# Stores of ScalarE's results begun from ScalarE's queue, and z's first two token blocks side by side

## The chip, the cores and the metric

The kernel runs on one core of a Trainium2 chip. The core has a matrix engine (TensorE, PE in the profile), three engines for elementwise work (VectorE or DVE, ScalarE or ACT, GpSimd or POOL), a queue engine (SyncE or SP) that here only begins transfers, and 16 DMA engines that move data between the chip's memory (HBM) and the core. Every engine works through its own list of instructions in the order in which the program gives them; a semaphore makes an instruction wait for another engine's result. A DMA is begun by an instruction on some engine's list, and that engine goes on as soon as the transfer is handed over.

The metric is the device time of one execution in microseconds (us). Three runs of the kernel before gave 1551.68, 1552.48 and 1552.88 us, so the median is 1552.48 us.

## What is computed

One layer of a decoder with two token mixers side by side, 1024 tokens of width 1024, all in float32:

```python
h = rms_norm(x, norm_w)
q, k, v, z_a, xbc, z_s, dt_raw, gate_logits = split(h @ w_in)   # 1024 x 11296
# branch A: attention with two softmax maps per head, 8 heads
y_a = diff_attention(q, k, v, ...) * silu(z_a)
# branch B: a state space scan in chunks of 128 tokens, 32 heads in 4 groups
xbc = silu(causal_depthwise_conv(xbc, conv_w, conv_b))
y_s = ssd_chunked(xs, dt, A, B, C, D)
y_s = gated_group_rms_norm(y_s, z_s, ssd_norm_w)                 # y * silu(z_s)
# merge
g_a, g_s = split(gate_logits)
merged = sigmoid(g_a) * (y_a @ w_proj_attn) + sigmoid(g_s) * (y_s @ w_proj_ssd)
out = x + merged @ w_out
```

Nearly all the time goes into the matrix products with w_in, w_proj_attn, w_proj_ssd and w_out. Each float32 factor is split into a high and a low part of a faster format, and a product is three matmuls: high times high, high times low, low times high.

## The kernel before

**A planner writes the order.** The kernel's Python code holds a small model of the engines (class Plan). Each step is a generator that emits instructions and yields the time at which it wants to go on; the planner keeps a clock for TensorE (pl.t) and one each for ScalarE ("A"), VectorE ("V"), GpSimd ("G"), SP's queue ("Q") and the DMA engines ("D"), and runs whatever is due. So the order of instructions on every engine's list is fixed when the program is built, by the model's costs. The function load (line 278) begins every DMA of the kernel but two, loads and stores alike, on SP's list. A store is emitted at the model's time at which its data are done.

**The front.** Tokens are worked on in eight blocks of 128 (t = 0 to 7). prep_h normalises a block: a square sum on ScalarE, a root on GpSimd, a scaling on VectorE, eight 128x128 transposes on TensorE (ph in the profile), then h_evac copies the high part to hH on ScalarE and the low part to hL on VectorE. The first products are those of z (z_first, line 1299; "y0" in the list of the order, FRONT_ORDER): for a token block t it multiplies the first half of the inner dimension (four slices kb, 12 matmuls, called "half 0" here) into a bank of PSUM; z_copy (line 1323) then copies that sum to a tile zc on ScalarE and stores it; then the second half (12 more matmuls, "half 1") is added in the same bank, and z_evac (line 1476) applies Silu and stores the result. The second half may not begin before the copy is done, since it goes on adding in the bank that is being read. Kept sums serve the later products of z by a scheme with seven products in place of eight (z_part, z_step), which fetch zc from HBM and may put changed sums back (z_keep, line 1334).

For the first pair of columns (pr = 0) z_first works on the blocks in the order (0), (1), (2, 3): block 0 alone, block 1 alone, blocks 2 and 3 together. Together means half 0 of both, then half 1 of both. After the first group it starts consts, which loads twelve small tables through SP's queue.

**Later stages.** From about 88 us to 540 us follow the products of gates (front_pair with kind g, gate_step), of the convolution's input (kind c; conv, line 1444) and the remaining products of z; from about 330 us the scan (ssd_core, ssd_chunk) runs beside them and goes on beside the attention (att_proj, att_block) from 557 us; then the last gates (gates, gate_evac) to about 1237 us, the products with w_proj (products) and with w_out (final).

**The stores that the change touches.** In att_block the tile yt (attention's result, transposed, last written on ScalarE); in z_keep the tile zc, from z_copy last written by ScalarE, and from z_step the tiles zu and zv last written by VectorE; in conv the tile cv after its Silu on ScalarE; in z_evac the tile zs or zu after its Silu; in gate_evac the tile gt after its Tanh. There are 48 stores of cv, 32 of z_evac, 24 of z_keep, 16 of yt and 12 of gt, each of 128 x 512 float32 (256 KB).

In front_pair a bank is used again after ScalarE has copied it: product p = 1 fills a bank, ScalarE copies it to fc, product p = 6 follows in another bank, and p = 2 goes on in the first one, which needs the copy ("ct").

Of the kernel before, what the change touches and what calls it, by code (L numbers as in the profile page):

```python
# [15 lines left out]
P = 128  # L16
# [137 lines left out]
def tile_hybrid_layer(ctx: ExitStack, tc: tile.TileContext, x, norm_w, w_in, q_norm_w, k_norm_w,  # L154
                      diff_lambda, subln_w, conv_w, conv_b, dt_bias, a_log, d_skip, ssd_norm_w,
                      w_proj_attn, w_proj_ssd, w_out, out):
    nc = tc.nc
# [14 lines left out]
    ya_d = dram.tile([1024, S], F32, name="ya_d")  # L172
    ys_d = dram.tile([2048, S], F32, name="ys_d")
    gt_d = dram.tile([2048, S], F32, name="gt_d")
    act_d = dram.tile([NT, SH, P], F32, name="act_d")
    acc_d = dram.tile([2048, 512], F32, name="acc_d")
    cv_d = dram.tile([3072, S], F32, name="cv_d")
    z_d = dram.tile([GROUPS, S, 512], F32, name="z_d")
# [3 lines left out]
    zc_d = dram.tile([2, 2, 512, 512], F32, name="zc_d")  # L182

    pl = Plan()
# [10 lines left out]
    def midt(shape=(P, 512), dt=F32, name="m"):  # L195
        return mid.tile(list(shape), dt, tag="b2", name=name)
# [39 lines left out]
    def pe_done():  # L236
        return pl.t + DONE
# [11 lines left out]
    def act(o, i, f, after, **kw):  # L249
        nc.scalar.activation(o, i, f, **kw)  # L250
        if f in (AF.Silu, AF.Exp) and f != table[0]:
            table[0] = f
            pl.op("A", 1.3, after)
        c = 0.83e-3 * i.free_size() + (0.052 if in_ps(i) else 0.093) + 0.093 * (("accum_out" in kw) + any(not isinstance(kw.get(i, 0.0), float) for i in ("scale", "bias")))
        return pl.op("A", c, after)
# [9 lines left out]
    def stt(o, a, s, b, op0, op1, after):  # L265
        nc.vector.scalar_tensor_tensor(out=o, in0=a, scalar=s, in1=b, op0=op0, op1=op1)
        sb = not in_ps(a, b)
        return pl.op("V", 0.07 + 0.07 * sb + 1.042e-3 * o.free_size() + (0.0 if isinstance(s, float) else 0.06), after, sb)
# [6 lines left out]
        nc.vector.tensor_copy(o, a)  # L275
        return pl.op("V", 0.065 + (1.042e-3 if in_ps(a) else 0.52e-3) * o.free_size(), after)

    def load(o, i, after=0.0):
        nc.sync.dma_start(out=o, in_=i)
        q = pl.op("Q", 0.48, max(after, pl.t))  # L280
        n = o.free_size() * 512 / 360e3 if o.space != bass.MemoryType.DRAM else i.free_size() * 512 / 360e3
        return pl.op("D", n, q + 0.6) + lag[1]

    def rsqrt(dst, src, add, after):
        cols = src.free_size()
        if isinstance(add, float):
            nc.gpsimd.tensor_scalar(out=dst, in0=src, scalar1=add, scalar2=None, op0=ALU.add)
        else:
            nc.gpsimd.tensor_tensor(out=dst, in0=src, in1=add, op=ALU.add)
        nc.gpsimd.tensor_tensor(out=dst, in0=dst, in1=mhalf[:, 0:cols], op=ALU.pow)  # L290
        return pl.op("G", 0.55 + 0.18 * cols, after)
# [100 lines left out]
    for kind, i in ORDER1:  # L392
# [8 lines left out]
        elif kind == "z":  # L401
            pr, p = divmod(i, 10)
# [196 lines left out]
    def w_next(n):  # L599
        i = used[0]  # L600
        used[0] += n
        return list(range(i, i + n))

    def w_need(i):
        while i not in w_at:
            yield pl.t + 0.1
        while w_at[i] > pl.t:
            yield w_at[i]

    def w_done(i):  # L610
        ws.give(w_slot[i], pl.t + 0.1)
        wts.pop(i)

    def wide(i):
        return wts[i][:, 0].rearrange("p f c -> p (f c)"), wts[i][:, 1].rearrange("p f c -> p (f c)")
# [5 lines left out]
    def steps3(o, a, b, first, last, **kw):  # L621
        mm(o, a[0], b[0], first, False, **kw)
        yield
        mm(o, a[0], b[1], False, False, **kw)
        yield
        mm(o, a[1], b[0], False, last, **kw)
        yield
# [215 lines left out]
    def hblk(kb, t):  # L843
        return hH[:, kb, t * P:(t + 1) * P], hL[:, kb, t * P:(t + 1) * P]
# [83 lines left out]
    def att_block(h, qb, pk, scs):  # L928
        v, zg, kk, ks = hd[h]
        n = (qb + 1) * P  # L930
# [32 lines left out]
        pr, sums = zip(*[got[m] for m in range(2)])  # L963
        at = max(ex)
# [6 lines left out]
        at = max(t1, t2)  # L971
        yield at
        nc.gpsimd.tensor_tensor(out=cc, in0=rec, in1=n0, op=ALU.mult)
        at = pl.op("G", 0.25, at)
        yield at
        at = stt(pr[0][:, 0:n], pr[1][:, 0:n], cc, pr[0][:, 0:n], ALU.mult, ALU.add, at - HOP)
# [30 lines left out]
        at = pe_done()  # L1007
# [4 lines left out]
        at = act(y, av[:, 0:P], AF.Square, at, accum_out=ss)  # L1012
        yield at
        f = tin(1, "f")
        at = rsqrt(f, ss, e1, max(at, t_e))
        yield at
        at = stt(y, av[:, 0:P], f, zg[:, qb, :], ALU.mult, ALU.mult, at)
# [13 lines left out]
        yt = yts[qb // 4]  # L1031
# [3 lines left out]
        at = pe_done()  # L1035
        yield at
        sms.give(kx, at)
        at = act(yt[0][:, (qb % 4) * P:(qb % 4 + 1) * P], py[:, 0:P], AF.Copy, at, scale=sub_c)
        trs.give(k, at)
        yt[2] += 1  # L1040
        if yt[2] == 4:
            yield at
            at = load(ya_d[h * P:(h + 1) * P, qb // 4 * 512:qb // 4 * 512 + 512], yt[0], at)
            ytm.give(yt[1], at)
            ready.setdefault("att", []).append(at)

# [251 lines left out]

    def z_first(pr):
        ids = w_next(KB)  # L1300
        for ts in (((0, 1), (2, 3)) if pr else ((0,), (1,), (2, 3))):
            pms = []
            for t in ts:
                k = yield from pl.get(trs, first=True)
                pms.append((mmt(f"pmz{pr}{t}"), k))
            for half in range(2):
                for t, (pm, k) in zip(ts, pms):
                    while half and (pr, t) not in z_c:
                        yield pl.t + 0.1
                    for kb in range(half * 4, half * 4 + 4):  # L1310
                        yield from w_need(ids[kb])
                        while (t, half) not in h_at:
                            yield pl.t + 0.1
                        while h_at[t, half] > pl.t:
                            yield h_at[t, half]
                        yield from steps3(pm, hblk(kb, t), wide(ids[kb]), kb == 0, kb % 4 == 3, skip_group_check=True)
                        if t == 3:
                            w_done(ids[kb])
                    pl.spawn(z_evac(2 * pr, t, pm, k, False) if half else z_copy(pr, t, pm), pe_done())
            if pr == 0 and ts[0] == 0:  # L1320
                pl.spawn(consts())

    def z_copy(pr, t, pm):
        at = pe_done()
        km = yield from pl.get(mids)
        c = midt(name=f"zc{pr}{t}")
        at = act(c, pm, AF.Copy, at)
        z_c[pr, t] = at
        yield at
        z_keep(pr, 0, t, c, km, at, False)  # L1330
# [2 lines left out]

    def z_keep(pr, n, t, o, km, at, keep):
        if not keep:
            at = load(zc_d[pr, n, t * P:(t + 1) * P], o, at)
            mids.give(km, at)
            o = None
        z_u[pr, n, t] = (o, km, at)
# [104 lines left out]
    def conv(b, h, ps, cell, at, free=None):  # L1444
        km = yield from pl.get(mids)
        cv = midt(name=f"cv{h}")
        yield max(at, pl.t)
        if h == 0:
            tail = tin(3, "tail")
            cell["tail", b] = (tail, act(tail, ps[:, 509:512], AF.Copy, at))  # L1450
        at = act(cv, ps, AF.Identity, at, bias=cbc(b), scale=cwc(3, b))
        for j in (1, 2, 3):
            yield at
            yield from pl.room("V")
            at = stt(cv[:, j:512], ps[:, 0:512 - j], cwc(3 - j, b), cv[:, j:512], ALU.mult, ALU.add, at)
        if h:
            while ("tail", b) not in cell:
                yield pl.t + 0.1
            tail, t = cell["tail", b]
            at = max(at, t)  # L1460
            for j in (1, 2, 3):
                yield at
                yield from pl.room("V")
                at = stt(cv[:, 0:j], tail[:, 3 - j:3], cwc(3 - j, b), cv[:, 0:j], ALU.mult, ALU.add, at)
        yield at
        if free:
            free[0].give(free[1], at)
        at = act(cv, cv, AF.Silu, at)
        cell["conv", b, h] = at
        yield at  # L1470
        at = load(cv_d[b * P:(b + 1) * P, h * 512:h * 512 + 512], cv, at)
        mids.give(km, at)
        cv_at[b, h] = at


    def z_evac(g, t, pm, k, own, at=None):
        at = pe_done() if at is None else at
        if own:
            zz, km = own
        else:  # L1480
            km = yield from pl.get(mids)
            zz = midt(name=f"zs{g}{t}")
        at = act(zz, pm, AF.Silu, at)
        trs.give(k, at)
        yield at
        at = load(z_d[g, t * P:(t + 1) * P, :], zz, at)
        mids.give(km, at)
        z_at[g, t] = at

# [221 lines left out]
    def gate_evac(ob, n, pm, k):  # L1711
        at = pe_done()
        km = yield from pl.get(mids)
        gt = midt(name=f"gt{ob}{n}")
        at = act(gt, pm, AF.Tanh, at, scale=0.5)
        trs.give(k, at)
        yield at
        at = load(gt_d[ob * P:(ob + 1) * P, n * 512:(n + 1) * 512], gt, at)
        mids.give(km, at)


# [529 lines left out]
```

## Time and profile before

| | |
|---|---|
| median of three runs | 1552.48 us |
| the profiled execution's own time | 1552.03 us |
| its span, first to last instruction | 1550.0 us |
| TensorE busy | 1534.9 us, 99% |
| VectorE busy | 1131.5 us, 73% |
| ScalarE busy | 887.6 us, 57% |
| GpSimd busy | 806.9 us, 52% |
| moved by DMA | 289.56 MB, 187 GB/s on average |

All times below are counted from the start of the span. The profile calls an instruction by its engine, its line in the kernel, the operation and the tiles that it writes and reads ("zc<-pmz"). A line can be that of a helper: L250 is every ScalarE operation, L218 every matmul, L279 every DMA begun through load. "Busy" for TensorE is what the trace models: matmuls overlap, and the distance from one start to the next tells the pace. The idle time of an engine is put down to what released it. Instructions that only begin a DMA are listed under the queue (SPq, ACTq) and are not counted as busy.

### The profile page before, as it was taken

The numbers are of one execution on the slowest core, as the hardware profiler recorded it, in microseconds if no ns is written. First come the engines' busy times: TensorE is split into PE (matmuls) and PEld (weight loads), VectorE is DVE, ScalarE is ACT, GpSimd is POOL, SyncE is SP. The second block draws the span as 40 slices with busy tenths as digits, with TensorE's granted clock in tenths as the row PEclk, the third lists the DMA queues.
The fourth block names the chain that finished last, engine by engine and source line by source line (L and its number), as shares of the span: only waits on it lengthen the run. The fifth ranks groups of instructions, "written<-read, shape, count | busy, mean of one in ns | idle before, by whom it ended". The sixth has DMA issues, their size and how long they took to land.

```text
span 1550.0 us, 26098 instructions
## 1 busy us (share of the span) xinstructions
PE 1534.9 (99%) x8562; PEld 1253.3 (81%) x8562; DVE 1131.5 (73%) x2091; ACT 887.6 (57%) x2203; POOL 806.9 (52%) x922
## 2 busy tenths in 40 slices
PE   7999999999999999999999999999999999999999
PEld 5887888888888878787878887888878888888887
DVE  6757978657688776877677777777456687888985
ACT  8654434355666666767766776766556555352350
POOL 3276376544555545455685645574768754322005
PEclk9999999999999999999999999999999999999999
DMA  7576678666544472324463424152438679698836
GB/s 237 172 222 215 218 254 292 205 200 224 187 143 130 133 215 77 117 77 143 153 204 117 150 76 135 62 174 82 157 137 264 228 275 315 227 333 262 308 130 224
DMA packets 255977, 289.56 MB, mean 187 GB/s; under 512 B 18519, under 2 KB 162656, under 8 KB 255842
## 3 DMA queue, kind: packets, MB, share of 16 engines
q1 hardware_dynamic: 255838, 287.89, 57.4%
q8 instruction: 68, 1.11, 0.3%
q14 instruction: 67, 0.55, 0.1%
q10 hardware_dynamic: 4, 0.00, 0.0%
HBM read 198.57 MB, written 89.26 MB: 186 GB/s over the span
## 4 chain that ended last, share of the span: by engine, by line
PE 91%; POOL 2%; DVE 2%; ACT 2%; DMA 2%; issue 1%; SPq 0%; POOLq 0%; DVEq 0%; ACTq 0%
PE pma L218 21%; PE pz L218 11%; PE fYc L218 6%; PE py L218 5%; PE fXc L218 4%; PE sc L218 4%; PE fZc L218 4%; PE av L218 4%; PE fYg L218 3%; PE px L218 3%; PE pO L218 3%; PE pg L218 3%; PE pmz L218 2%; PE pa L233 2%; PE poz L218 1%; PE fZg L218 1%
## 5 line engine op out<-in xcount | busy, mean ns | idle before, releaser
L218 PE MATMUL pma<-w,hH 128*128 128x512 f32 x1024 | 347.4, 407 | 0.6 <-ACT at L250 0.6
L218 PEld LDWEIGHTS pma<-w,hH 128*128 128x128 f32 x1024 | 186.9, 188 | 40.6 <-issue 5.5
L218 PE MATMUL pma<-w,hL 128*128 128x512 f32 x512 | 208.4, 407 | 0.0
L250 ACT ACTIVATE w<-raw 128x512 fp32r<-128x512 f32 (+1 forms) x166 | 102.5, 630 | 65.3 <-DMA raw<-wf_d 25.1
L218 PEld LDWEIGHTS pma<-w,hL 128*128 128x128 f32 x512 | 96.6, 189 | 20.0 <-issue 3.0
L258 POOL TENSOR_TENSOR rawf<-rawf,rawf 128x512 f32<-128x512 f32 x54 | 70.6, 1307 | 79.8 <-DVE wp L258 37.2
L258 DVE TENSOR_TENSOR w<-raw,w 128x512 fp32r<-128x512 f32 (+1 forms) x114 | 91.0, 810 | 23.8 <-ACT w L250 23.6
L250 ACT ACTIVATE p<-p,nm 128x256 f32<-128x256 f32 (+7 forms) x128 | 98.2, 769 | 17.1 <-DVE nm L946 13.8
L218 PE MATMUL fYc<-ft,wp 128*128 128x512 f32 x432 | 105.6, 391 | 0.0
L218 PEld LDWEIGHTS fYc<-ft,wp 128*128 128x128 f32 x432 | 80.6, 188 | 16.7
L258 POOL TENSOR_TENSOR w<-raw,w 128x512 fp32r<-128x512 f32 x52 | 69.9, 1350 | 41.2 <-ACT w L250 41.2
L218 PE MATMUL pz<-w,ft 128*128 128x512 f32 x384 | 91.3, 392 | 0.0
L250 ACT ACTIVATE wp<-rawp 128x512 fp32r<-128x512 f32 x72 | 44.5, 628 | 76.6 <-POOL rawp L258 18.2
L258 POOL TENSOR_TENSOR rawp<-rawp,rawp 128x512 f32<-128x512 f32 x36 | 52.7, 1469 | 59.8 <-DVE wp L258 50.8
L218 PEld LDWEIGHTS pz<-w,ft 128*128 128x128 f32 x384 | 71.5, 188 | 14.7
L250 ACT ACTIVATE ab<-ab,nac 128x128 f32<-128x128 f32 x256 | 78.4, 395 | 2.2 <-POOL ab L1503 1.7
L946 DVE CUSTOM_DVE_ANT_0 p<-sc,maskb 128x512 f32<-128x512 f32 (+3 forms) x128 | 69.1, 585 | 13.5 <-PE sc L218 13.3
L218 PEld LDWEIGHTS av<-v,at 128*128 128x128 f32 x576 | 73.3, 191 | 4.5 <-issue 0.4
L290 POOL TENSOR_TENSOR rs<-rs,mhalf 128x4 f32<-128x4 f32 (+1 forms) x71 | 73.1, 1030 | 5.9
L258 POOL TENSOR_TENSOR os<-os,os 128x512 f32<-128x512 f32 x48 | 68.9, 1436 | 13.4 <-DMA os<-in_w_in_dram 5.4
L218 PE MATMUL av<-v,at 128*128 128x128 f32 x576 | 75.4, 275 | 0.0
L250 ACT ACTIVATE wp<-rawf 128x512 fp32r<-128x512 f32 x100 | 60.1, 624 | 23.0 <-POOL rawf L258 20.6
(376 smaller groups left out, 4171.1 us busy)
## 6 DMA issues: line engine op xcount, KB each, us to landing
raw<-in_w_in_dram SPq DMA_DIRECT2D x104, 256.0 KB, 3.2
rawf<-in_w_in_dram SPq DMA_DIRECT2D x72, 256.0 KB, 3.8
ab<-act_d SPq DMA_DIRECT2D x32, 512.0 KB, 5.3
wf_d<-os SPq DMA_DIRECT2D x48, 256.0 KB, 2.3
cv_d<-cv SPq DMA_DIRECT2D x48, 256.0 KB, 2.5
raw<-wf_d SPq DMA_DIRECT2D x48, 256.0 KB, 3.2
t_d<-ts SPq DMA_DIRECT2D x24, 512.0 KB, 2.7
os<-in_w_in_dram SPq DMA_DIRECT2D x32, 256.0 KB, 5.2
```

The costliest lines, as they stand in the source:

```text
L218: nc.tensor.matmul(o, lhsT=lhsT, rhs=rhs, start=start, stop=stop, **kw)
L233: nc.tensor.transpose(out=o, in_=i, identity=ident if idn is None else idn)
L250: nc.scalar.activation(o, i, f, **kw)
L258: (nc.vector if eng == "V" else nc.gpsimd).tensor_tensor(out=o, in0=a, in1=b, op=op)
L290: nc.gpsimd.tensor_tensor(out=dst, in0=dst, in1=mhalf[:, 0:cols], op=ALU.pow)
L946: nc.vector.tensor_tensor_reduce(out=p[:, j:e], in0=sc[m][:, o:o + e - j], in1=maskb[:, S - n + j:S - n + e], scale=-1.0, scalar=nms[i - 1 ...
```

## The change

load gets a switch: with own=True the DMA is begun from ScalarE's list, and the planner books 0.35 us on ScalarE's clock for it in place of 0.48 us on SP's. Five calls set it: those in att_block, z_keep, conv, z_evac and gate_evac. The other stores (among them those of gate_out, gate_copy, final_store and the scan) stay on SP. And z_first takes the blocks as (0, 1), (2, 3) for both pairs of columns.

```diff
-    def load(o, i, after=0.0):
-        nc.sync.dma_start(out=o, in_=i)
-        q = pl.op("Q", 0.48, max(after, pl.t))
+    def load(o, i, after=0.0, own=False):
+        (nc.scalar if own else nc.sync).dma_start(out=o, in_=i)
+        q = pl.op("A", 0.35, max(after, pl.t)) if own else pl.op("Q", 0.48, max(after, pl.t))
...
-            at = load(ya_d[h * P:(h + 1) * P, qb // 4 * 512:qb // 4 * 512 + 512], yt[0], at)
+            at = load(ya_d[h * P:(h + 1) * P, qb // 4 * 512:qb // 4 * 512 + 512], yt[0], at, own=True)
...
-        for ts in (((0, 1), (2, 3)) if pr else ((0,), (1,), (2, 3))):
+        for ts in ((0, 1), (2, 3)):
...
-            at = load(zc_d[pr, n, t * P:(t + 1) * P], o, at)
+            at = load(zc_d[pr, n, t * P:(t + 1) * P], o, at, own=True)
...
-        at = load(cv_d[b * P:(b + 1) * P, h * 512:h * 512 + 512], cv, at)
+        at = load(cv_d[b * P:(b + 1) * P, h * 512:h * 512 + 512], cv, at, own=True)
...
-        at = load(z_d[g, t * P:(t + 1) * P, :], zz, at)
+        at = load(z_d[g, t * P:(t + 1) * P, :], zz, at, own=True)
...
-        at = load(gt_d[ob * P:(ob + 1) * P, n * 512:(n + 1) * 512], gt, at)
+        at = load(gt_d[ob * P:(ob + 1) * P, n * 512:(n + 1) * 512], gt, at, own=True)
```

## The prediction

> **What bounds the kernel now.** I read the page's list of engines first, then the table by stages, then what TensorE waits for.
>
> ```profile
> span 1550.0 us, 26098 instructions
> PE 1534.9 (99%) x8562; PEld 1253.3 (81%) x8562; DVE 1131.5 (73%) x2091; ACT 887.6 (57%) x2203; POOL 806.9 (52%) x922
> ```
> ```profile
> 0.00:50.00 50.00, 42.03 (x191) 31.81 (x192) 35.86 (x62) 41.28 (x76) 14.91 (x31) 1.00 0.70 232
> 50.00:550.00 500.00, 500.00 (x2407) 410.60 (x2405) 365.31 (x576) 262.61 (x511) 271.47 (x218) 1.00 0.63 200
> 550.00:1250.00 700.00, 697.18 (x4650) 566.39 (x4649) 488.55 (x1099) 465.58 (x1408) 428.30 (x608) 1.00 0.45 145
> 1250.00:1538.00 288.00, 287.58 (x1276) 237.69 (x1275) 238.51 (x352) 118.11 (x209) 87.58 (x63) 1.00 0.77 258
> ```
>
> After a stretch's length these rows give the busy time of PE, PEld, DVE, ACT and POOL. TensorE is idle for 7.97 us of the first 50, for none of the next 500, for 2.82 of the 700 with the attention, and for 0.42 until 1538. So nothing that only makes another engine or a queue shorter can give more than those idle times. The granted clock is 1.00 throughout, so none of it is a slower clock. What can be won stands in the waits of TensorE:
>
> ```profile
> PE pmz L218 <- ACT zc L250: 4.0, 2, 2.0
> PE px L233 <- DVE cv L266: 1.1, 1, 1.1
> ```
>
> The columns are total, times and longest. Half of the front's idle time is two waits of z's first product for the copy of its own first half; the largest in the attention is 1.1 us.
>
> **Part 1: blocks 0 and 1 side by side.** What these waits are, the front shows on PE, ACT and DVE:
>
> ```profile
> 14.74 0.40 PE L218 MATMUL pmz<-w,hL 128*128 128x512 f32 x1
> 17.07 0.72 PE L218 MATMUL pmz<-w,hH 128*128 128x512 f32 x2 [1.94 <-ACT zc L250]
> 24.18 0.40 PE L218 MATMUL pmz<-w,hL 128*128 128x512 f32 x1
> 26.60 0.73 PE L218 MATMUL pmz<-w,hH 128*128 128x512 f32 x2 [2.02 <-ACT zc L250]
> 15.47 1.06 ACT L250 ACTIVATE hH<-ph 128x512 fp32r<-128x512 f32 x2
> 16.42 0.60 ACT L250 ACTIVATE zc<-pmz 128x512 f32<-128x512 f32 x1
> 16.21 1.28 DVE L258 TENSOR_TENSOR hL<-ph,hH 128x512 fp32r<-128x512 f32 x2
> 28.19 1.28 DVE L258 TENSOR_TENSOR hL<-ph,hH 128x512 fp32r<-128x512 f32 x2
> ```
> ```profile
> 28.03 0.44 PE ph L233 x4
> 55.50 21.76 PE pmz L218 x96
> ```
>
> Half 0 of block 0 ends at about 15.0; half 1 waits for the copy and starts at 17.07. The same happens at 24.4, to 26.60. In the new order half 0 of block 1 comes into the first gap. It is not free to start at 15.0: its high part ends on ACT at about 16.0 (first of the two from 15.47), its low part on DVE at about 16.9 (first of the two from 16.21), and the third matmul needs the low part. So the wait for the copy gives way to a wait for block 1's own data, and the first gap shrinks little. From there the steps are, at 21.76/96 = 0.227 us for a matmul: the third matmul at 16.9 and ten in all to 19.2; half 1 of block 0, 12 x 0.227 = 2.7, to 21.9, its copy done since 17.0; 16 transposes of blocks 2 and 3, which stood in the same stretch before, 4 x 0.44 = 1.8, to 23.7; then half 1 of block 1, whose copy has had four microseconds. It started at 26.60 and now starts at 23.7: **2.9 us won**. Bounds: 4.0, both waits gone, and nothing, if what follows isn't there earlier.
>
> Is it there? Block 2 is now wanted at 23.7 + 2.7 + 0.9 (eight more transposes) = 27.3, block 3 at about 30. Block 3's low part was made by 28.8 and 29.4 (the last DVE row), so it just holds. But ScalarE, which feeds all this, is busy for 41.28 of the first 50 us, and now gets the stores of zc and zs of four blocks on top, eight of 0.33 us or more. I take off 0.5 and keep **2.4 us**. Behind 60 us TensorE never pauses until 550, so what is won there is carried to the end: the weights come by a ring that follows TensorE's own use.
>
> **Part 2: the stores.** What moves, counted:
>
> ```profile
> cv_d<-cv SPq DMA_DIRECT2D x48, 256.0 KB, 2.5
> z_d<-zs SPq DMA_DIRECT2D x16, 256.0 KB, 2.3
> z_d<-zu SPq DMA_DIRECT2D x16, 256.0 KB, 2.0
> ya_d<-yt SPq DMA_DIRECT2D x16, 256.0 KB, 4.8
> gt_d<-gt SPq DMA_DIRECT2D x12, 256.0 KB
> L279 SPq DMA_DIRECT2D zc_d<-zc x8: 319/329/2373, 20.2 to 72.5; - x8
> L279 SPq DMA_DIRECT2D zc_d<-zu x8: 319/320/373, 157.6 to 300.6; - x8
> L279 SPq DMA_DIRECT2D zc_d<-zv x8: 319/320/384, 190.8 to 352.5; - x8
> ```
>
> Together 132 stores (the last rows give the least, median and longest issue in ns). SP loses them, ScalarE gets 132 x 0.33 = 44 us of issues beside 888 busy, and after each it can't go on until its own result is written. SP's gain:
>
> ```profile
> SPq L279 <- ACT cv L250: 82.0, 36, 11.8
> SPq L279 <- ACT yt L250: 53.0, 10, 11.8
> SPq L279 <- ACT gt L250: 21.1, 8, 6.4
> SPq L279 <- DVE zu L258: 6.6, 4, 4.3
> ```
>
> SP stood over 150 us at the head of its list before such stores, with loads queued behind. But TensorE felt at most the 2.82 us of the middle, and its largest wait there is for DVE, not for a load. I cost SP's relief at **nothing**; the bounds are 3.2 us won (2.82 + 0.42, every wait gone) and nothing.
>
> The Trainium skill has a rule here (DMA: Bandwidth & Descriptors, Issuing engines are not separate DMA queues): beginning DMAs from several engines only saves the time that the sequencer takes to begin them. By it the stores are worth SP's issue time, which does not bound this kernel, and part 2 gains nothing; by the waits above it could still save a queue from standing behind another engine's work.
>
> ScalarE's loss: in the products of gates and conv (88 to 550 us) TensorE goes on in a bank that ScalarE has copied, one form of 12 matmuls (2.7 us) later:
>
> ```profile
> L250 ACT ACTIVATE fc<-fXc x12: 575/598/602, 110.0 to 536.5; 128x512 f32<-128x512 f32 x12
> ```
>
> The copy takes 0.6, so some 2 us are spare; a store ahead of it takes 0.33 and about 0.1 for the result to be written, and is covered. Where the cover is short, it isn't: a tile zu or zv of z_keep is last written by DVE, and SP waited up to 4.3 us for one; ScalarE would stand there with the copies of the banks queued behind it, and 4.3 - 2 = 2.3 us would reach TensorE. Four waits in 16 stores, 6.6 in all, say rarely. Bounds: nothing, and all of the 6.6. By the 12 copies, the nearest row, I take **0.6 us** lost.
>
> **Sum.** 1552.03 (this execution's own time, 0.45 under the median) - 2.4 + 0 + 0.6 = 1550.2 us, 0.15% under the median.
>
> **Rival A, slower: ScalarE is held by a slot.** SP's waits include landings of other DMAs. At the last gates the store of gt had its data long before it began:
>
> ```profile
> 1190.96 0.60 ACT L250 ACTIVATE gt<-pg 128x512 f32<-128x512 f32 x1 [1.32 <-PE pg L218]
> 1193.62 0.60 ACT L250 ACTIVATE kk<-pq 128x512 fp32r<-128x512 f32 x1 [0.91 <-PE pq L233]
> 1195.37 1.25 PE L218 MATMUL sc<-kk,q 64*128 64x512 f32 x12
> 1197.56 0.33 SPq L279 DMA_DIRECT2D gt_d<-gt  x1
> 1238.88 0.58 ACT L250 ACTIVATE gt<-pg 128x512 f32<-128x512 f32 x1
> 1247.61 1.07 ACT L250 ACTIVATE at<-pa 128x512 f32<-128x512 f32 x2
> 1249.75 1.95 PE L218 MATMUL av<-v,at 128*128 128x128 f32 x16
> 1245.16 0.32 SPq L279 DMA_DIRECT2D gt_d<-gt  x1
> ```
> ```profile
> SPq L279 <- DMA os<-in_w_out_dram: 0.5, 2, 0.3
> ```
>
> The first gt was ready at 1191.56 and begun at 1197.56, the second at 1239.46 and 1245.16; the last row (SP's waits from 1239 to 1246) has DMAs that wait for an earlier load to land. My reading is that only so many DMAs may be under way and a new one waits for an old one's place. On SP that costs nothing. On ScalarE it stops the engine for 5.7 to 6.0 us, with kk queued behind the first, and the splits of weights and at behind the second. kk stands behind that store (to 1197.9) and one more copy, 0.5, and would begin at 1198.4 instead of 1193.62, 4.8 later; its low part is one DVE step like that of hL, 0.64, so that sc has some 0.4 to spare: 4.4 lost. at would come 5.7 later, av had 1.1 to spare: 4.6 lost. Both: 1550.2 + 9.0 = **1559.2**; one alone gives about 1554.7. It decides from the point at which such a store meets a full set of loads. For it: the loads there (the forms for the products, w_proj, w_out) start just as the last gates end. Against: the order is planned anew, and with SP not held by gt the loads go earlier.
>
> **Rival B: the front gives nothing.** ScalarE is full there, and the longest issue of the zc row, 2.37 us, is the first one, at 20.2, with x and weights under way. If an issue holds ScalarE so long, twice, blocks 2 and 3 come later by as much as was won: 1552.03 + 0.6 = **1552.6**. The skill's page Perfetto Trace Analysis (DMA Instruction — HWDGE) says that the two queues share one generator of descriptors and that a DMA's recorded time holds the wait for it; by that rule ScalarE would pay SP's long issues too, and this rival would hold. No row here shows two queues in conflict.
>
> **Rival C: the loads were late after all.** With SP free, the waits of the middle go: 1550.2 - 3.2 = **1547.0**.
>
> **The change doesn't do what it says** for the 16 stores of zu and zv: these are DVE's results. That is in the 0.6 above.
>
> **How the numbers follow.** The forecast, 1548.6 to 1551.8 by itself, has 0.38; rival C 0.20, A 0.30, B 0.12. A measurement here tells about 0.2% from no change, 3.1 us: faster is under 1549.4, slower over 1555.6. Faster: all of C and 0.14 of the forecast, 0.34. Slower: A at both places, 0.26. Same: 0.24 of the forecast, B, and A at one place, 0.40. The range goes from 1546.5, just under C, to 1559.5, A in full; about 0.05 is left out below and 0.1 above. The order is planned anew from the first block on, so small waits of the middle can come and go: that is in these edges, as 1 to 2 us either way.
>
> **What would show it.** Right: no row of pmz waiting for zc, half 1 of block 1 from about 23.7, every later stage two to three us earlier (the gates e4 were at 44.6), the stretch from 50 to 550 without idle time. Part 2 free: TensorE's waits between 550 and 1250 still about 2.8. A: a wait of sc, av or px for ACT near 1195 or 1250, and ScalarE's queue waiting for a DMA before a store. B: waits of pmz for hH or hL of blocks 2 and 3, and long issues on ACTq. Wrong altogether I would be if a new wait on ScalarE stood in the stretch without idle time, since there every microsecond counts in full.

## The result, and the profile after

| | before | after |
|---|---|---|
| median of three runs, us | 1552.48 | 1577.86 (1575.59 to 1578.2) |
| span of the profiled execution, us | 1550.0 | 1576.1 |
| TensorE idle in the span, us | 15.1 | 27.7 |

After takes 1.0155 of the time before, with a 95% interval of 1.0138 to 1.0172: 25 us slower. The prediction, 1550.2 with a range up to 1559.5, was wrong. The page of after, its list of engines, and the table by the same stages as before (after a stretch's length: busy time of PE, PEld, DVE, ACT and POOL, then the granted clock):

```profile
PE 1548.4 (98%) x8562; PEld 1256.6 (80%) x8562; DVE 1127.0 (72%) x2091; ACT 892.3 (57%) x2205; POOL 803.8 (51%) x922
```
```profile
0.00:50.00 50.00, 44.05 (x197) 32.76 (x198) 38.37 (x68) 41.99 (x79) 15.15 (x31) 1.00 0.72 231
50.00:550.00 500.00, 491.02 (x2370) 400.33 (x2369) 350.63 (x560) 258.40 (x497) 263.60 (x212) 0.99 0.62 197
550.00:1250.00 700.00, 697.30 (x4591) 563.45 (x4590) 480.22 (x1084) 458.27 (x1391) 423.19 (x606) 1.00 0.44 138
1250.00:1538.00 288.00, 281.74 (x1249) 231.58 (x1248) 238.64 (x356) 130.43 (x235) 79.77 (x60) 0.98 0.76 256
```

The front gained, as forecast: 44.05 us busy and 197 matmuls in the first 50, where it was 42.03 and 191. Then comes what was not forecast. From 50 to 550 us, where TensorE had not paused once, it is idle for 9 us; from 1250 on for 6 us in place of 0.4. And its busy time, for the same 8562 matmuls, is 13.5 us longer (1548.4 against 1534.9), so the matmuls themselves ran slower for a while. What TensorE waited for (total, times, longest; the rows that are new or that the forecast named):

```profile
PE pz L218 <- DVE f0b L258: 3.3, 2, 2.9
PE py L218 <- DVE nm L946: 2.6, 1, 2.6
PE pz L218 <- DVE w L258: 2.0, 1, 2.0
PE fXc L218 <- ACT wp L250: 1.9, 1, 1.9
PE fXc L218 <- DVE wp L258: 1.7, 2, 1.2
PE fYg L218 <- DVE wp L258: 1.6, 1, 1.6
PE pz L218 <- ACT w L250: 1.4, 1, 1.4
PE sc L218 <- ACT kk L250: 1.3, 1, 1.3
PE pmz L218 <- ACT zc L250: 0.3, 1, 0.3
```

The two waits of pmz for zc, 4.0 us before, are down to 0.3. The eight rows above it did not stand among the waits of before; five of them are for VectorE, three for ScalarE. The earliest of them, near 155 us (pz for w, first ScalarE's, then VectorE's), is seen on the lists of VectorE and ScalarE and then of TensorE in after (start, duration, instruction, and in brackets the idle time before it with what ended it):

```profile
152.75 0.70 DVE L258 TENSOR_TENSOR fZc<-fu,fZc 128x512 f32<-128x512 f32 x1 [1.70 <-PE fZc L218]
154.34 0.42 DVE L266 SCALAR_TENSOR_TENSOR tv<-tv,tv 128x256 f32<-128x256 f32 x1
154.68 0.74 DVE L266 SCALAR_TENSOR_TENSOR cv<-fZc,cols,cv 128x511 f32<-128x511 f32 x1
155.34 0.42 DVE L266 SCALAR_TENSOR_TENSOR tv<-tv,tv 128x256 f32<-128x256 f32 x1
155.67 0.74 DVE L266 SCALAR_TENSOR_TENSOR cv<-fZc,cols,cv 128x510 f32<-128x510 f32 x1
...
157.98 0.68 DVE L258 TENSOR_TENSOR w<-raw,w 128x512 fp32r<-128x512 f32 x1
155.12 0.33 ACTq L279 DMA_DIRECT2D cv_d<-cv  x1
155.50 0.63 ACT L250 ACTIVATE w<-raw 128x512 fp32r<-128x512 f32 x1 [0.40 <-ACT cv L250]
```
```profile
156.18 0.50 PE L218 MATMUL pz<-w,ft 128*128 128x512 f32 x1 [1.43 <-ACT w L250]
158.72 1.80 PE L218 MATMUL pz<-w,ft 128*128 128x512 f32 x6 [2.04 <-DVE w L258]
```

and on the lists of VectorE and ScalarE in before, at the same place of the work:

```profile
153.66 0.68 DVE L258 TENSOR_TENSOR fZc<-fu,fZc 128x512 f32<-128x512 f32 x1
154.26 0.41 DVE L266 SCALAR_TENSOR_TENSOR tv<-tv,tv 128x256 f32<-128x256 f32 x1
154.59 0.68 DVE L258 TENSOR_TENSOR w<-raw,w 128x512 fp32r<-128x512 f32 x1
152.32 0.62 ACT L250 ACTIVATE w<-raw 128x512 fp32r<-128x512 f32 x1
```

It is the same work in another order. Before, the low part of z's next weight (w) stood two places behind the sum fZc, 0.9 us later. In after, four steps of the convolution (cv) and six of the time-step table (tv) stand between them, 5.2 us; TensorE is through with fZc and waits. The high part of the same weight, on ScalarE, is late too: before it came ahead of the sum, at 152.32, and in after behind the convolution's Silu and the begin of its store, at 155.50. That begin, 0.33 us, is the only part of a store in this stall. The planner had booked 132 stores on ScalarE's clock instead of SP's, and so every list was planned anew.

Rival A is there as well, on ScalarE's list of after:

```profile
1202.76 0.60 ACT L250 ACTIVATE gt<-pg 128x512 f32<-128x512 f32 x1 [0.68 <-PE pg L218]
1208.74 0.33 ACTq L279 DMA_DIRECT2D gt_d<-gt  x1
1209.12 0.60 ACT L250 ACTIVATE kk<-pq 128x512 fp32r<-128x512 f32 x1 [4.99 <-DMA rawp<-in_w_proj_ssd_dram]
```

The store of gt held ScalarE, with kk queued behind it, until a load of w_proj had landed. So two causes are at hand, the order and the queue, and a run that changes both cannot say how much belongs to which. The chain that ended last does not say it either: 91% of it is TensorE, before and after.

### The profile page after: what moved, and what is told of

Read it like the earlier page. It is cut to its first block, busy times and chain, and to the rows that moved or that the text cites. A ratio compares the mean times of both kernels' runs of the same rounds, so it can differ in the third digit from the quotient of the medians.

```text
span 1576.1 us, 26021 instructions
## 1 busy us (share of the span) xinstructions
PE 1548.4 (98%) x8562; PEld 1256.6 (80%) x8562; DVE 1127.0 (72%) x2091; ACT 892.3 (57%) x2205; POOL 803.8 (51%) x922
## 4 chain that ended last, share of the span: by engine, by line
PE 91%; DMA 4%; DVE 2%; ACT 1%; issue 1%; POOL 1%; SPq 0%; ACTq 0%; DVEq 0%; POOLq 0%
PE pma L218 22%; PE pz L218 11%; PE fYc L218 6%; PE py L218 6%; PE fZc L218 4%; PE fXc L218 4%; PE sc L218 4%; PE av L218 4%; PE px L218 3%; PE pO L218 3%; PE fYg L218 3%; PE pa L233 2%; DMA raw<-in_w_in_dram 2%; PE pg L218 2%; PE fXg L218 1%; PE poz L218 1%
## 5 line engine op out<-in xcount | busy, mean ns | idle before, releaser
L250 ACT ACTIVATE w<-raw 128x512 fp32r<-128x512 f32 (+1 forms) x166 | 101.5, 627 | 56.7 <-DMA raw<-in_w_in_dram 11.2
L258 POOL TENSOR_TENSOR os<-os,os 128x512 f32<-128x512 f32 x48 | 66.3, 1382 | 15.4 <-DMA os<-in_w_in_dram 11.2
```

What stands on the lines that cost most here:

```text
L258: (nc.vector if eng == "V" else nc.gpsimd).tensor_tensor(out=o, in0=a, in1=b, op=op)
```

## The experiments

The theories: **order** (the loss comes from the new order of the lists), **queue** (ScalarE is held by stores), and, for part 1, whether its 2.4 us last to the end. Times are medians; each ratio is to runs of the kernel before on the same chip, with its 95% interval.

**e1, before's order, the stores on ScalarE's queue.** In the planner a store is still booked on SP, so that the lists of TensorE, VectorE and GpSimd are instruction for instruction those of before. Against before (own=True at the five calls, as in the change):

```diff
-        nc.sync.dma_start(out=o, in_=i)
+        (nc.scalar if own else nc.sync).dma_start(out=o, in_=i)
         q = pl.op("Q", 0.48, max(after, pl.t))
```

> The order of before, with nothing changed on TensorE, VectorE and GpSimd; only the 132 stores are begun from ScalarE's queue (the planner still books them on SP, and z's blocks 0 and 1 are one after the other). Theory order (the 25 us come from the new order that the planner makes, not from the queue): 1551 to 1554, before within 0.2%, with a stall of sc or av at the last gates of at most 2 us. Theory queue (ScalarE is held by stores that wait for the landing of an older DMA or for VectorE): 1565 or more, with waits for ACT in the stretch from 150 to 550.

Measured: 1558.78 us, 1.0040 (1.0027 to 1.0054), 5.6 us slower. It lies between the two forecasts, nearer to that of order, with a stall larger than "at most 2 us". ScalarE's list and TensorE's windows:

```profile
1191.89 0.60 ACT L250 ACTIVATE gt<-pg 128x512 f32<-128x512 f32 x1 [0.74 <-PE pg L218]
1197.88 0.33 ACTq L279 DMA_DIRECT2D gt_d<-gt  x1
1198.25 0.69 ACT L250 ACTIVATE q<-pq,cols 128x512 fp32r<-128x512 f32 x1 [5.77 <-DMA rawp<-in_w_proj_ssd_dram]
```
```profile
1195.00:1200.00 5.00, 2.38 (x13) 1.33 (x13) 1.02 (x2) 1.69 (x3) 3.43 (x4) 1.00 1.17 310
1200.00:1205.00 5.00, 4.97 (x20) 3.79 (x19) 2.77 (x10) 2.34 (x6) 2.17 (x3) 0.66 0.61 227
```

ScalarE does nothing for 5.77 us; TensorE loses 2.6 us in the first window, and in the next one its granted clock is 0.66, another 0.34 x 5 = 1.7 us. Followed matmul by matmul against before, the kernel falls back by 4.7 us here, 1.1 near 1255, and 2.2 in the front, of which 1.2 are back before 1180. In the front two new waits of pmz for zc stand (1.2 together), and the first transposes begin 0.75 us later; whether the stores are to blame this run leaves open. In the full stretch from 50 to 550 it has no idle time at all.

**e2, after's order, the stores on SP's queue.** The counterpart, against after:

```diff
-        (nc.scalar if own else nc.sync).dma_start(out=o, in_=i)
+        nc.sync.dma_start(out=o, in_=i)
         q = pl.op("A", 0.35, max(after, pl.t)) if own else pl.op("Q", 0.48, max(after, pl.t))
```

> The order of after, with nothing changed on TensorE, VectorE and GpSimd; only the 132 stores go back to SP's queue (the planner still books them on ScalarE). Theory order: it keeps most of the loss, 1570 to 1580, with the stalls near 155 (pz), 475 (fXc) and 1258 and 1295 (py, pz) in place; the stall of sc near 1209 goes, 2 us. Theory queue: the stalls go with the stores, 1549 to 1556.

Measured: 1575.20 us, 1.0142 (1.0120 to 1.0164), 22 us slower than before. TensorE's waits:

```profile
PE pz L218 <- DVE f0b L258: 3.3, 2, 2.9
PE pz L218 <- DVE w L258: 2.6, 1, 2.6
PE py L218 <- DVE nm L946: 2.4, 1, 2.4
PE fXc L218 <- DVE wp L258: 1.8, 2, 1.2
PE fXc L218 <- ACT wp L250: 1.8, 1, 1.8
```

These are after's stalls at the same places, without one store on ScalarE; of the large ones only the wait of sc for kk is gone. The order makes most of the loss.

**e3, part 1 alone.** Only the line of z_first is changed against before:

```diff
-        for ts in (((0, 1), (2, 3)) if pr else ((0,), (1,), (2, 3))):
+        for ts in ((0, 1), (2, 3)):
```

> Part 1 alone: z's blocks 0 and 1 side by side, all stores on SP and booked there. By the trace of after the front gains 2.2 us, so that 1550.3 is expected if the order of the rest holds (my prediction's step for part 1, carried to the end). Theory order in its wide form (any edit that moves the plan brings new stalls in the full stretch): a stall of TensorE of over 1 us between 50 and 550, and 1552 to 1565.

Measured: 1550.74 us, 0.9983 (0.9973 to 0.9992): 2.4 us faster, with no idle time from 50 to 550. The planner kept most of before's order, so that the stretch without pauses survived.

**e4, part 2 alone.** After with the line of z_first as it was before.

> Part 2 alone: the 132 stores begun from ScalarE's queue and booked there, z's blocks 0 and 1 one after the other. Theory order: the new order comes from the booking, so that most of the loss is here, 1568 to 1582. If the loss of after needs both parts together (a coincidence of the two), 1552 to 1560.

Measured: 1581.35 us, 1.0178 (1.0160 to 1.0196). The loss needs no coincidence of the two parts.

Does booking on ScalarE make the order bad, or does any new order lose? **e5 and e6** are controls that change nothing on the chip but the order: the kernel before, stores on SP, with another figure in the planner for what beginning a DMA takes (e5 as below; e6 with 0.46).

```diff
-        q = pl.op("Q", 0.48, max(after, pl.t))
+        q = pl.op("Q", 0.50, max(after, pl.t))
```

> The kernel before, every store on SP, z's blocks as they were: only the planner's figure for what beginning a DMA takes on SP is 0.50 in place of 0.48, so that it plans another order. Theory re-plan (before's order is an unusually good one among near ones, and what costs is that the order is made anew, whatever the reason): slower by 0.5 to 1.5%, 1560 to 1576, with stalls of TensorE of 1 us and more that before hasn't, at places of their own. Theory booking (the order gets worse because 44 us more are booked on ScalarE): within 0.3% of before, 1549 to 1557.

> As the kernel with 0.50, on the other side: the figure is 0.46. Theory re-plan: slower here too, 1558 to 1576, at other places than with 0.50. Theory booking: within 0.3% of before. If a smaller figure were simply truer or falser than a larger one, the two would lie on two sides of before.

Measured: e5 1569.11 us, 1.0112 (1.0091 to 1.0133); e6 1580.25 us, 1.0175 (1.0160 to 1.0190). A figure moved by 0.02 us in either direction costs 16 and 27 us, the second as much as the whole change, and 4 us more than the upper edge of what was expected for it. Of TensorE's waits, first e5, then e6:

```profile
PE pma L218 <- DVE pre L258: 3.0, 1, 3.0
PE av L218 <- ACT at L250: 1.4, 1, 1.4
```
```profile
PE poa L218 <- DVE w L258: 8.2, 1, 8.2
PE pO L218 <- DVE ab L258: 3.1, 2, 3.0
PE pma L218 <- POOL w L258: 2.8, 1, 2.8
```

Other waits, at other places (near 788 us in e5; 541, 808 and 1489 in e6), of the same kind: an operand made late because other work stood ahead of it in an engine's list. Theory booking falls as the sole cause: nothing was booked on ScalarE here.

**e7, the whole change, planned with other figures.** All 132 stores on ScalarE's queue and booked there, blocks side by side; against after:

```diff
-        q = pl.op("A", 0.35, max(after, pl.t)) if own else pl.op("Q", 0.48, max(after, pl.t))
+        q = pl.op("A", 0.3041, max(after, pl.t)) if own else pl.op("Q", 0.4711, max(after, pl.t))
```

The two figures are no better measured than the others; they were picked because the planner then books fewer pauses for TensorE.

> After in all that it does on the chip (the 132 stores begun and booked on ScalarE, z's blocks side by side), but planned with 0.304 in place of 0.35 for a store on ScalarE and 0.471 in place of 0.48 for a DMA on SP: another order of the same work. Theory re-plan: another time, and as this order was chosen from many for few stalls in the plan, a better one: 1555 to 1566, at least 10 us under after. Theory booking: the same loss as after, 1570 to 1582.

Measured: 1559.98 us, 1.0044 (1.0028 to 1.0061). The same change on the chip, 18 us faster than after, by the order alone.

What do the stores themselves cost? **e8 to e10** keep the lists of part 1 alone (e3) on TensorE, VectorE and GpSimd and move stores only: all but gt (e8), gt alone (e9), all (e10). **e11** is after with only gt's 12 stores put back on SP, its booking unchanged. The edit of e8, against e3 with own=True at the five calls and e1's line in load:

```diff
-        at = load(gt_d[ob * P:(ob + 1) * P, n * 512:(n + 1) * 512], gt, at, own=True)
+        at = load(gt_d[ob * P:(ob + 1) * P, n * 512:(n + 1) * 512], gt, at)
```

> The order of part 1 alone (TensorE, VectorE and GpSimd as in the run of part 1 alone), with 120 stores begun from ScalarE's queue: all but the 12 of gt. The run with before's order and all stores on ScalarE lost 6 us, 4.5 of them near 1196, where the store of gt held ScalarE for 5.8 us until a load had landed, and about 1 near 1255. If the slot behind gt is what the queue costs (my rival A): 1550 to 1553, the time of part 1 alone, with no stall of sc near 1195. If the other stores hold ScalarE too: 1555 or more.

> The order of part 1 alone, unchanged on TensorE, VectorE and GpSimd; only the 12 stores of gt are begun from ScalarE's queue. If rival A is the whole cost of the queue: 1554.5 to 1557, with ScalarE idle for 5 to 6 us before a store of gt, a stall of sc of 2 to 3 us near 1195, and the granted clock at about 0.66 in the 5 us after it (1.7 us more). If it needed the other stores too (their places among the transfers under way): 1550 to 1552.

> The order of part 1 alone, with all 132 stores begun from ScalarE's queue (booked on SP): what the change would be if the order were kept. By the runs so far the sum is part 1's gain of 2.4 and the slot behind gt, 4.5 to 6: 1554 to 1558. If SP's relief is worth something beside it: 1550 to 1553.

> The order of after, unchanged on TensorE, VectorE and GpSimd; only the 12 stores of gt go back to SP. In after the store at 1208.7 held ScalarE with kk behind it (stalls of sc of 1.7 and 0.7 and a clock of 0.66 for 5 us): 3 to 4 us back, 1573 to 1576, as with all stores on SP (1575.2). If the slot does nothing there: 1577 to 1579.

| run | us | ratio to before (95%) |
|---|---|---|
| e3, no store moved | 1550.74 | 0.9983 (0.9973 to 0.9992) |
| e8, 120 stores, not gt | 1551.09 | 0.9988 (0.9979 to 0.9997) |
| e9, gt's 12 alone | 1558.25 | 1.0037 (1.0022 to 1.0052) |
| e10, all 132 | 1558.72 | 1.0040 (1.0027 to 1.0054) |
| e11, after's order, gt on SP | 1570.55 | 1.0122 (1.0103 to 1.0140) |

Twelve stores cost all of it; the other 120 cost and gain nothing that these runs can tell. e9 and e10 came out up to 1.3 us above what was expected, e11 2.5 us below. ScalarE's and TensorE's lists of e9, then e9's windows:

```profile
1189.13 0.60 ACT L250 ACTIVATE gt<-pg 128x512 f32<-128x512 f32 x1 [1.25 <-PE pg L218]
1195.94 0.33 ACTq L279 DMA_DIRECT2D gt_d<-gt  x1
1196.31 0.69 ACT L250 ACTIVATE q<-pq,cols 128x512 fp32r<-128x512 f32 x1 [6.58 <-DMA rawp<-in_w_proj_ssd_dram]
1197.05 2.18 PE L218 MATMUL sc<-kk,q 64*128 64x512 f32 x12 [3.39 <-ACT q L250]
```
```profile
1195.00:1200.00 5.00, 2.95 (x14) 2.35 (x15) 2.61 (x7) 1.69 (x3) 2.54 (x2) 0.70 1.06 378
1200.00:1205.00 5.00, 5.00 (x15) 3.92 (x15) 2.07 (x9) 3.76 (x10) 1.83 (x3) 0.62 0.14 54
```

and ScalarE's list of e8 at the same place, where SP stores gt:

```profile
1189.13 0.60 ACT L250 ACTIVATE gt<-pg 128x512 f32<-128x512 f32 x1 [0.74 <-PE pg L218]
1190.26 0.69 ACT L250 ACTIVATE q<-pq,cols 128x512 fp32r<-128x512 f32 x1 [0.53 <-PE pq L233]
```

Both tiles gt begin at the same time; q begins 1.1 us after that in e8 and 7.2 in e9, where the store stands in front of it.

## Why the prediction was wrong, point by point

**Where the 25.4 us are.** Order: e2 less e3, both with all stores on SP, 24.5 us lost. Part 1: e3, 2.4 won. In after's order, the 120 stores: e11 less e2, 4.6 won, though the intervals of these two still overlap; gt's twelve: after less e11, 1.0155 against 1.0122, 8.0 lost by the differences to before (25.4 less 17.4). The sum is 24.5 - 2.4 - 4.6 + 8.0 = 25.5; it closes because each run is taken off the next, so it is no check. Nor are the last two shares shown to come from the stores alone. Followed matmul by matmul, after ends 8.4 us behind e11. Of these, 3.8 stand near 1210, where gt's store held ScalarE; 1.4 near 480 and 2.0 near 1262 stand where both runs have the stall and the clock fell in after alone (0.75 and 0.76 in its first window there, 1.00 in e11). Likewise e2 ends 3.5 us behind e11, with 1.5 of it in the first 50 us and 1.0 behind the stall near 155, where the window from 160 to 165 has a clock of 0.50 in e2 and of 0.82 in e11.

**What bounds the kernel: right.** TensorE at 99%, with no idle time over 500 us. What I read from it, that nothing which only shortens another engine can gain, held: e8's 120 stores gain nothing.

**Part 1: right in mechanism, and near in size.** I had 2.4 us kept; e3 gives 2.4 by medians (1.2 to 4.2 by the interval), and its waits of pmz for zc are gone. One execution alone shows the size badly: TensorE's first wait for x was 1.2 us in before and 2.4 in e3, and its 301st matmul began at 74.8 and 74.9 us. Over all profiled executions that matmul began between 73.1 and 74.9 us in the eight with blocks 0 and 1 side by side, 74.0 on average, and between 74.8 and 77.2 in the five without, 76.1 on average. The step itself came later than forecast: half 1 of block 1, from 23.7 by my sum, began at 24.5 in after and at 25.6 in e3.

**Part 2, SP's relief at nothing: right where the order stands** (e8 against e3). The Trainium skill's rule that I weighed (DMA: Bandwidth & Descriptors, Issuing engines are not separate DMA queues: beginning DMAs from several engines saves only the sequencer's time to begin them) agrees with that: 120 stores moved, 0.35 us of difference. Whether it is worth something in after's order, the 4.6 above leave open.

**Part 2, ScalarE's loss of 0.6: not contradicted for 120 of the 132 stores, wrong for gt's twelve.** For the 120, e8 lies 0.35 over e3, which these runs can't tell from nothing or from 0.6. The twelve were rival A, which I had at 0.30 and not in the sum. Its mechanism is what the runs show: a store whose data were done waits until an earlier load has landed, and on ScalarE that holds all behind it (6.58 us idle in e9). Its total of 9.0 for both places came near the 7.5 measured (e9 less e3), but by luck, with two errors against each other: the second place, priced at 4.6, cost 1.4 in e9, and the first, priced at 4.4, cost 6.5, since I had not priced the slower clock after the stall (3.4 us in the two windows of e9 above).

**The step that failed: "the order is planned anew from the first block on, so small waits of the middle can come and go: that is in these edges, as 1 to 2 us either way".** It cost 24.5. I worked out every edit on the trace of before, as if the lists stayed as they were but for the moved instructions. But the lists are an output of the planner, and a booking of 0.35 us on another clock changes them all. The controls show how little is needed: 0.02 us in one figure, with no change in what is done, and 16 or 27 us are lost. Of the orders run here, before's (with that of part 1, which keeps most of it) is the best by 7 us and more, though e7 pays for its stores in that. Full use of the busiest engine, which I read as "what is won is carried to the end", was also the warning that there is nothing for a worse order to hide in. A stretch at 100% has only one way to go.

I had named the sign of this error, a new wait in the stretch without idle time, but looked for it on ScalarE behind a store. Most of it stood on VectorE's list, where the change adds nothing (11.2 us in the five rows above), and the part on ScalarE's list before 550 us, 3.3 us, is there in e2 as well, without a store (2.7).

**Rivals B and C: neither.** e8 has zc's stores on ScalarE and keeps the front's gain, 0.9988 of before (against B), and with SP free nothing was won (against C). In after ScalarE's eight begins of zc took 0.39 us at most, where B feared 2.37, and its 48 begins of cv 0.33 in the median and 0.47 at most, so no conflict of the two queues is seen in them.

**The best version here** is part 1 alone, 0.9983 of before and faster than both kernels by the interval. Whether another order near it is better still was not tried.

## What to carry to other kernels

Where a planner writes the order, an edit to what it books is a change of everything behind it: measure that part by itself, by keeping the booking while changing the instruction, and the instruction while changing the booking, and run one control that moves only a figure, to see how far the time scatters without any real change. Put a store on the queue of an engine that computes only where the transfers under way leave room for it when its data are done: look in the profile for begins that come long after their data. A wait of TensorE of two to three microseconds should be priced with what the clock may take after it, 1.7 us or more where it fell here.

## What the runs showed of the hardware

**After a stall, TensorE can run at a lower clock for some microseconds.** Windows of after, each stall with the five microseconds behind it:

```profile
155.00:160.00 5.00, 1.78 (x7) 1.25 (x8) 4.93 (x12) 0.72 (x2) 0.00 (x0) 1.00 0.18 58
160.00:165.00 5.00, 5.00 (x17) 3.95 (x16) 3.68 (x10) 3.09 (x5) 1.27 (x1) 0.66 0.81 254
1295.00:1300.00 5.00, 1.86 (x4) 1.34 (x5) 4.79 (x5) 1.44 (x3) 3.04 (x2) 0.67 0.92 338
1300.00:1305.00 5.00, 5.00 (x16) 3.88 (x15) 3.16 (x5) 2.71 (x5) 0.00 (x0) 0.65 0.14 54
```

In the second row TensorE has no idle time and yet starts 17 matmuls, where the stretch from 50 to 550 before averaged 24 in five microseconds (2407 in 500). A mean of 0.66 over 5 us is what 3.4 us at half speed would give (0.5 x 3.4 = 0.34 x 5), and no window of any run here lies under 0.50. The Trainium skill (TensorE: Matmul & The Clock Gate, What's actually happening) says that the clock falls to one half after an idle window of about 3.4 us and comes back after as long a busy one. The length of the slow time agrees; but pauses shorter than 3.4 us were enough here, 2.6 us in e1. Not every such pause does it: one of 2.4 us at 1256 in e2 left the clock at 1.00, and the two of 1.9 and 0.5 us near 476 brought it down in after but not in e11. What decides is not shown. Over after, the five-microsecond windows behind 50 us with a clock under 1 add up to 10 us, about two fifths of the loss and most of the 13.5 us by which TensorE's busy time grew, and in the profile of before there is none but that of the last few microseconds.

**A DMA begun on ScalarE's queue can wait for a load on SP's.** The store of gt in e9 began within 0.1 us of the landing of the load that stands eight DMAs earlier in the program, and so did others on both queues. The instruction records of the traces name a completion semaphore for each DMA: there are eight of them for all 1076 DMAs, handed out in turn over both queues, and this store has the same one as that load. So my reading is that the two queues share the places for transfers under way, eight of them in this program; that the number decides was not tried by an experiment.
